# Layer 0 of a streaming encoder step: copying a chunk's first output part behind its first product, and reading sample states when their pair's values are made

## The chip, the cores and the metric

The kernel runs on one core of one Trainium2 chip. The metric is the time of one launch in microseconds (us) of device time, as the median of several runs. Engines are named as in the profile: PE is the matrix engine (PEld its weight loads), DVE the vector engine, ACT the scalar engine, POOL GpSimd, and SP the engine whose queue issues the DMAs.

## The reference, cut to what matters

Two layers are computed for 512 prompt tokens and 32 sample tokens. Layer 0 mixes tokens with RWKV-7: each of 24 heads keeps a 64 x 64 state that is updated token by token.

```
def step(S, inp):
    r_t, k_t, v_t, w_t, kk_t, a_t = inp
    sa = jnp.einsum('bhvk,bhk->bhv', S, -kk_t)
    S = (S * w_t[:, :, None, :] + sa[..., None] * (kk_t * a_t)[:, :, None, :]
         + v_t[..., None] * k_t[:, :, None, :])
    return S, jnp.einsum('bhvk,bhk->bhv', S, r_t)
xs = tuple(jnp.swapaxes(t, 0, 1) for t in (r, k, v, decay, kk, a))
S_T, y = lax.scan(step, S0.astype(f32), xs)
```

The prompt starts from a zero state, the sample from `state_rwkv`, one 64 x 64 matrix for each head. Both final states are outputs. Layer 1 is differential attention. Each layer has an input projection, a memory cross-attention, a gate and an output projection; these projections are most of the arithmetic.

## The kernel before, in words

**Tiling.** All tokens stand side by side as 544 columns (512 + 32). A projection block is 128 output columns: its weights are loaded (tiles `raw`), split into a high part by ACT (`whi`) and a low part by DVE (`wlo`), and multiplied in three products for each of 8 slices of the model dimension, over two halves of 272 columns (PSUM tile `ps_g`).

**The recurrence.** The 24 heads are 12 pairs; a pair fills the 128 partitions. The scan over tokens is replaced by chunks of 64 tokens: 8 prompt chunks in a row for a pair, and one sample chunk (number 8) with its own state. `rw_prep` makes the operands of a pair, `rw_values` the part of the chunks' values that needs no state (`avz`), `rw_chain` and `rw_sample` run the chunks through `chunk`, `rw_outputs` adds the rest of the outputs, `rw_finish` normalizes.

**A chunk**, with its PSUM tile `ps_c` (one bank, four parts), goes in three steps that follow each other through the engines; the names are those of the profile:

1. The first product `ps_c<-SB,zr` (PE) multiplies the state (`SB`, for the sample `ssi`) by the chunk's operands. One half of its rows is added by DVE to `avz` (`avz<-ps_c,avz`). The other half is the chunk's first output part.
2. The second product `ps_c<-avz,at` (PE) follows. ACT copies its result out in two copies (`sv<-ps_c`, for the sample `svs<-ps_c`), then copies the first output part of step 1 into the output tile (`yt<-ps_c`), then scales the old state (`sd<-SB,dl`).
3. The third product `ps_c<-sv,bt` (PE) and DVE's `SB<-ps_c,dl,sd` make the new state.

**Order.** Steps are Python generators. A hand-written table (`PLAN`, 23 rows of two halves) says in which place of a pair's chain the other steps of this and of neighbouring pairs are issued; between them the projection stream (`stream`) is filled in, a few matmuls at a time, so that PE has work while DVE and ACT finish a step. Each engine executes its instructions in the order in which the code issues them. In the plan, `rw_values` of pair p+1 is begun in row 22 of pair p and ended in row 1 of pair p+1; `rw_sample` is begun in row 5.

**The sample state.** The first thing that `rw_sample` does is to issue the two DMAs that read a pair's two matrices into the tile `SS`; right behind, in the same place of the plan, PE transposes `SS` (`ps_si<-ident,SS`), and DVE copies the result to `ssi`. After the sample chunk `SS` receives the new state, PE transposes it (`ps_so<-ident,SS`), and it is written out.

Of the kernel before, what the change touches and what calls it, by code (L numbers as in the profile page):

```python
# [108 lines left out]
class Trunk:  # L109
# [810 lines left out]
    H = [slice(0, 64), slice(64, P)]  # L920
# [8 lines left out]

    def rw_values(self, st):  # L930

        avz, H = self.avz, self.H
        for sets in (((0, 8),), ((1, 3, 5, 7), (2, 4, 6))):
            yield
            ps = [self.psm.tile([P, 4, P], F32, tag="m", name=f"ps_v{cs[0]}") for cs in sets]
            for j in range(len(sets[0])):
                for h in range(2):
                    for q, cs in zip(ps, sets):
                        if j < len(cs):
                            _, zs, ro, A, cv, _ = self.place(st, cs[j])  # L940
                            self.te.matmul(q[zs, j, H[h]], A[0][ro, h, :], cv[ro, H[h]], start=True, stop=True)
            for q, cs in zip(ps, sets):
                e, zs = self.place(st, cs[0])[:2]
                i = slice(0, 5, 4) if cs[0] == 0 else slice(cs[0] // 2, 4)
                self.ae.copy(avz[zs, e, i, :], q[zs, : len(cs)])
# [8 lines left out]
    def chunk(self, st, c, S, Snew):  # L954

        nc, H, yt = self.nc, self.H, st["yt"]
        e, zs, ro, A, cv, cb = self.place(st, c)
        i = c // 2
        yield
        ps = self.psc.tile([P, 4, P], F32, tag="c", name="ps_c")  # L960
        rhs = self.avz[:, e, i, :]
        sd = None
        if c:
            self.te.matmul(ps[:, 0, :], st["zr"][:, c * P : c * P + P], S[:], start=True, stop=True)
            self.ve.tensor_tensor(rhs[zs], ps[zs, 0, :], rhs[zs], ALU.add)
            yield

        self.te.matmul(ps[:, 1, :], A[0].rearrange("p h t -> p (h t)"), rhs, start=True, stop=True)
        for h in range(2):
            self.ae.copy(cv[zs, H[h]], ps[H[h], 1, H[h]])  # L970
        if c:
            self.ae.copy(yt[ro, i, :], ps[ro, 0, :])
            sd = self.rb2.tile([P, P], F32, tag="sd", name="sd", bufs=RB)
            self.ae.activation(sd[:], S[:], AF.Copy, scale=st["dl"][:, c : c + 1])
        yield
        self.te.matmul(ps[:, 2, :], cb, cv, start=True, stop=True)
        for hc in H:
            d = st["dl"][hc, c : c + 1]
            if c == 0:
                self.ve.tensor_scalar(Snew[hc, hc], ps[hc, 2, hc], d, None, ALU.mult)  # L980
            else:
                self.ve.scalar_tensor_tensor(Snew[hc, hc], ps[hc, 2, hc], d, sd[hc, hc], ALU.mult, ALU.add)
# [11 lines left out]
    def rw_sample(self, st):  # L994

        nc, p, pr = self.nc, self.rb2, st["pr"]
        sl = self.SS[0]
        for h in range(2):
            self.se.dma_start(sl[64 * h : 64 * h + 64, 64 * h : 64 * h + 64], self.a["state_rwkv"][0, 0, 2 * pr + h])
        yield  # L1000
        ps = self.psm.tile([P, 4, P], F32, tag="m", name="ps_si")
        self.te.transpose(ps[:, 0, :], sl[:], self.ident[:])
        S = p.tile([P, P], F32, tag="ssi", name="ssi", bufs=1)
        self.ve.tensor_copy(S[:], ps[:, 0, :])
        yield from self.chunk(st, 8, S, sl)
        yield
        self.state_out(sl, self.o[8][0, 0, 2 * pr : 2 * pr + 2])
# [1241 lines left out]
```

## Time and profile before

| | |
|---|---|
| median of 3 runs | 1373.17 us (1372.61 to 1374.08) |
| the profiled execution | 1373.67 us |
| its span in the trace | 1371.9 us, so 1.8 us lie around it |
| PE busy | 1343.1 us |
| PEld busy | 1289.0 us |
| DVE busy | 932.7 us |
| ACT busy | 827.6 us |
| POOL busy | 379.0 us |

The profile is of one execution. Layer 0's chunks lie between 133 and 660 us of the span. Row times in a timeline are the start from the span's beginning in us and then the duration in us; in brackets stands the idle time of that engine ahead of the instruction and what ended it.

### The profile page before, as it was taken

The page shows a single profiled execution, that of the slowest core. Times are in us where ns is not written, and L with a number is a line of the kernel's source. Part 1 is how long each engine was busy: PE and PEld are TensorE (multiplying, and loading weights), DVE is VectorE, ACT ScalarE, POOL GpSimd, SP SyncE. Part 2 cuts the span into 40 slices and gives each one's busy share as a digit, 9 for nine tenths or more (in the row PEclk, how much of TensorE's full clock was granted, in tenths as well). Part 3 has the DMA queues.
Part 4 walks back from the last instruction along what each step waited for, and adds up shares of the span by engine and source line. Part 5 has one row for each costly group of instructions (what it writes and reads, how often), then busy time and mean ns, then how long its engine had stood idle before and what let it go on. Part 6 is the DMA issues. An engine that isn't in the chain of part 4 may idle for free.

```text
span 1371.9 us, 31923 instructions
## 1 busy us (share of the span) xinstructions
PE 1343.1 (98%) x11893; PEld 1289.0 (94%) x11893; DVE 932.7 (68%) x2345; ACT 827.6 (60%) x2304; POOL 379.0 (28%) x841
## 2 busy tenths in 40 slices
PE   8999999999999999999999999999999999999997
PEld 6988899999999998988999999999999999999997
DVE  5776788888888888667734666775567747667443
ACT  5766777877778777656433466654566536665222
POOL 2128667766686666600000120000000001002000
PEclk9999999999999999999999999999999999999999
DMA  6452322333323332432644463333333323332321
GB/s 221 145 142 70 77 68 60 94 86 74 88 68 84 92 83 65 138 91 74 199 140 122 145 194 93 97 102 86 101 94 94 89 82 93 98 97 78 93 79 72
DMA packets 264036, 139.45 MB, mean 102 GB/s; under 512 B 57721, under 2 KB 252802, under 8 KB 263882
## 3 DMA queue, kind: packets, MB, share of 16 engines
q1 hardware_dynamic: 263818, 137.41, 35.7%
q8 instruction: 94, 1.54, 0.5%
q14 instruction: 60, 0.49, 0.1%
q10 hardware_dynamic: 64, 0.02, 0.0%
HBM read 111.12 MB, written 22.91 MB: 98 GB/s over the span
## 4 chain that ended last, share of the span: by engine, by line
PE 87%; DVE 5%; ACT 3%; POOL 2%; issue 1%; DMA 1%; SPq 1%; DVEq 0%; ACTq 0%; POOLq 0%
PE ps_g L106 60%; PE ps_c L106 5%; PE ps_s L106 2%; PE ps_o L106 2%; PE ps_at L106 2%; PE ps_v L106 2%; PE ps_mo L106 1%; PE ps_mm L106 1%; PE ps_w L106 1%; PE ps_aT L106 1%; POOL tm L868 1%; POOL u L870 1%; PE ps_yc L106 1%; PE ps_mt L106 1%; PE ps_wa L106 1%
## 5 line engine op out<-in xcount | busy, mean ns | idle before, releaser
L106 PE MATMUL ps_g<-hh,whi 128*128 128x272 f32 x1808 | 539.6, 299 | 1.0 <-DVE ats L106 0.7
L106 PE MATMUL ps_g<-hh,wlo 128*128 128x272 f32 x1808 | 534.7, 296 | 1.6 <-DVE wlo L106 1.5
L106 PE MATMUL ps_g<-hl,whi 128*128 128x272 f32 x1808 | 532.5, 295 | 0.6 <-DVE hl L106 0.3
L106 PEld LDWEIGHTS ps_g<-hh,whi 128*128 128x128 f32 x1808 | 341.1, 189 | 5.1 <-DVE ats L106 0.9
L106 PEld LDWEIGHTS ps_g<-hh,wlo 128*128 128x128 f32 x1808 | 340.6, 189 | 4.7 <-DVE wlo L106 2.5
L106 PEld LDWEIGHTS ps_g<-hl,whi 128*128 128x128 f32 x1808 | 341.1, 189 | 2.8 <-DVE hl L106 1.3
L106 DVE TENSOR_TENSOR wlo<-raw,whi 128x512 fp32r<-128x512 f32 x314 | 220.0, 711 | 122.3 <-ACT whi L106 118.9
L106 ACT CAST whi<-raw 128x512 fp32r<-128x512 f32 x314 | 188.9, 619 | 108.5 <-PE ps_g L106 61.4
L868 POOL TENSOR_TENSOR tm<-u,m 102x84 f32<-102x84 f32 (+23 forms) x341 | 145.6, 427 | 117.1 <-DMA m<-sc 67.1
L870 POOL TENSOR_TENSOR u<-u,tm 102x84 f32<-102x84 f32 (+23 forms) x341 | 150.4, 441 | 26.6
L106 PE MATMUL ps_g<-hi,whi 128*128 128x272 f32 x512 | 148.9, 291 | 0.0
L106 PE MATMUL ps_g<-hi,wlo 128*128 128x272 f32 x512 | 147.5, 288 | 0.5 <-DVE wlo L106 0.5
L106 PE MATMUL ps_g<-lo,whi 128*128 128x272 f32 x512 | 147.4, 288 | 0.0
L1339 POOL TENSOR_TENSOR lo<-og,hi 128x544 fp32r<-128x544 f32 x8 | 13.2, 1651 | 359.6 <-ACT hi L106 359.1
L106 PEld LDWEIGHTS ps_g<-hi,wlo 128*128 128x128 f32 x512 | 96.4, 188 | 0.8 <-DVE wlo L106 0.7
L106 PEld LDWEIGHTS ps_g<-hi,whi 128*128 128x128 f32 x512 | 96.4, 188 | 0.0
L106 PEld LDWEIGHTS ps_g<-lo,whi 128*128 128x128 f32 x512 | 96.4, 188 | 0.0
L106 ACT ACTIVATE pt<-ps_s,snm 128x128 f32<-128x128 f32 (+3 forms) x96 | 50.9, 531 | 41.8 <-DVE snm L106 41.6
L1766 POOL TENSOR_TENSOR hl<-hn,hh 128x544 fp32r<-128x544 f32 x8 | 12.5, 1566 | 211.2 <-ACT hh L106 211.2
L106 DVE SCALAR_TENSOR_TENSOR SB<-ps_c,dl,sd 64x64 f32<-64x64 f32 x168 | 47.4, 282 | 26.4 <-PE ps_c L106 21.1
L106 ACT COPY sv<-ps_c 64x64 f32<-64x64 f32 x192 | 39.5, 206 | 32.8 <-PE ps_c L106 30.9
L106 ACT ACTIVATE sg<-ps_g 128x272 f32<-128x272 f32 x64 | 25.2, 394 | 41.1 <-PE ps_g L106 38.3
(402 smaller groups left out, 2576.9 us busy)
## 6 DMA issues: line engine op xcount, KB each, us to landing
raw<-in_rw_in_dram SPq DMA_DIRECT2D x114, 256.0 KB
raw<-in_df_in_dram SPq DMA_DIRECT2D x112, 256.0 KB
raw<-in_w_out_dram SPq DMA_DIRECT2D x64, 256.0 KB
oscr<-sg SPq DMA_DIRECT2D x16, 272.0 KB
lo<-oscr SPq DMA_DIRECT2D x16, 272.0 KB
m<-sc SPq DMA_DIRECT2D x33, 128.0 KB
raw<-in_w_mem_v_dram SPq DMA_DIRECT2D x16, 256.0 KB
kh<-kh SPq DMA_DIRECT2D x24, 136.0 KB
```

The lines of the kernel that those rows point to most:

```text
L106: return lambda *a, **k: self.trunk.tie(self, issue(*a, **k))
L868: nc.gpsimd.tensor_tensor(tm[:, :n, :wd], u3[:, :n, kx : kx + 1].to_broadcast(sh), m3[:, kx : kx + 1, kx + 1 :].to_broadcast(sh), ALU.mult)
L870: nc.gpsimd.tensor_tensor(u3[:, :n, kx + 1 :], u3[:, :n, kx + 1 :], tm[:, :n, :wd], ALU.add)
L1339: (self.nc.gpsimd if g % 2 and self.o1 else self.ve).tensor_tensor(lo[:], t, hi[:].bitcast(F32), ALU.subtract)
L1766: nc.gpsimd.tensor_tensor(self.hl[:, k, :], h[:], self.hh[:, k, :].bitcast(F32), ALU.subtract)
```

## The change

The change has two parts, and only moves instructions.

- The copy `yt<-ps_c` of the first output part is issued right behind DVE's `avz<-ps_c,avz` (step 1 of the chunk), ahead of the second product, where it stood behind the two `sv<-ps_c` copies. This concerns 96 copies: chunks 1 to 7 and the sample chunk of 12 pairs.
- The two DMAs of `SS` are issued at the beginning of `rw_values` of their pair, where they stood at the beginning of `rw_sample`.

```
     def rw_values(self, st):
 
-        avz, H = self.avz, self.H
+        avz, H, pr = self.avz, self.H, st["pr"]
+        for h in range(2):
+            self.se.dma_start(self.SS[0][H[h], H[h]], self.a["state_rwkv"][0, 0, 2 * pr + h])
         for sets in (((0, 8),), ((1, 3, 5, 7), (2, 4, 6))):
             yield
...
             self.te.matmul(ps[:, 0, :], st["zr"][:, c * P : c * P + P], S[:], start=True, stop=True)
             self.ve.tensor_tensor(rhs[zs], ps[zs, 0, :], rhs[zs], ALU.add)
+            self.ae.copy(yt[ro, i, :], ps[ro, 0, :])
             yield
 
         self.te.matmul(ps[:, 1, :], A[0].rearrange("p h t -> p (h t)"), rhs, start=True, stop=True)
         for h in range(2):
             self.ae.copy(cv[zs, H[h]], ps[H[h], 1, H[h]])
         if c:
-            self.ae.copy(yt[ro, i, :], ps[ro, 0, :])
             sd = self.rb2.tile([P, P], F32, tag="sd", name="sd", bufs=RB)
...
         sl = self.SS[0]
-        for h in range(2):
-            self.se.dma_start(sl[64 * h : 64 * h + 64, 64 * h : 64 * h + 64], self.a["state_rwkv"][0, 0, 2 * pr + h])
         yield
```

On PE the sequence of matmuls stays; what the second product waits for is another engine. In pair 0, second chunk, the list of PE's instructions with what each waits for changes so (`ps_b` and `ps_g` are other work; a wait is named by the engine, or the DMA queue, whose semaphore it reads):

```order
 L106 MATMUL ps_b<-r_1904,hs_508 128x32
 L106 MATMUL ps_g<-hh,whi 128x272
-L106 MATMUL ps_c<-avz,at_89 128x128 [waits DMAHW2_49,DVE_49]
+L106 MATMUL ps_c<-avz,at_89 128x128 [waits DMAHW2_49,Activation_49]
 L106 MATMUL ps_g<-hl,whi 128x272
 L106 MATMUL ps_g<-hh,wlo 128x272
```

The second product waited for DVE's addition; now it waits for an instruction of ACT.

On ACT the copies move past 2 to 8 other instructions each. In pair 10 the last two chunks of the chain stood so (`t1b`, `at`, `mq`, `mp`, `mpT`, `hi`, `whi` are copies and activations of other steps):

```order
L106 CAST whi<-raw 128x512 [waits DMAHW4_49]
L106 COPY t1b<-ps_w_9771 32x256 [waits PE_49]
L106 COPY t1b<-ps_w_9771 32x256
L106 ACTIVATE mq<-ps_g 128x272 [waits PE_49]
L106 COPY sv<-ps_c 64x64 [waits PE_49]
L106 COPY sv<-ps_c 64x64
L106 COPY yt_1689<-ps_c 64x128
L106 ACTIVATE sd<-SB_538,dl 128x128 [waits Activation_49]
L106 COPY mpT<-ps_mt_9816 128x2x256 [waits PE_49]
L106 CAST hi_9332<-lo_9333 128x544 [waits DMAHW5_49]
L106 ACTIVATE mp,mrs<-ps_mm,mnm 128x256 [waits DVE_49,Activation_49]
L106 COPY mpT<-ps_mt_9870 128x2x256 [waits PE_49]
```

and now stand so:

```order
L106 CAST whi<-raw 128x512 [waits DMAHW4_49]
L106 COPY yt_1689<-ps_c 64x128 [waits DVE_49]
L106 COPY t1b<-ps_w_9772 32x256 [waits PE_49]
L106 COPY t1b<-ps_w_9772 32x256
L106 ACTIVATE mq<-ps_g 128x272 [waits PE_49]
L106 COPY sv<-ps_c 64x64 [waits PE_49]
L106 COPY sv<-ps_c 64x64
L106 ACTIVATE sd<-SB_538,dl 128x128 [waits Activation_49]
L106 COPY mpT<-ps_mt_9816 128x2x256 [waits PE_49]
L106 CAST hi_9334<-lo_9335 128x544 [waits DMAHW7_49]
L106 ACTIVATE mp,mrs<-ps_mm,mnm 128x256 [waits DVE_49,Activation_49]
L106 COPY yt_1689<-ps_c 64x128 [waits DVE_49]
```

The first copy has passed `t1b` and `mq`; the second, that of the next chunk, stands right behind `mp` and ahead of the second `mpT`. Each waits for DVE by itself, where it had no wait of its own behind `sv`.

On SP, where pair 10's state is read, the DMAs stood so (`cmt`, `mhk`, `mhv`, `cmv` are loads of the memory attention, `lo` of the output projection):

```order
L106 DMA oscr_476<-sg_83 128x544
L106 DMA cmt<-in_cache_mem_k_dram 128x2x128
L106 DMA mhk<-mkv_176 128x256
L106 DMA mhv<-mkv_779 128x256
L106 DMA cmv<-in_cache_mem_v_dram 128x2x128
L106 DMA raw<-in_rw_in_dram 128x4x128 x2
L106 DMA lo_9333<-oscr_475 128x544
L106 DMA lo_9382<-oscr_475 128x544
L106 DMA SS<-in_state_rwkv_dram 64x64 x2
```

and now stand so:

```order
L106 DMA oscr_476<-sg_83 128x544
L106 DMA SS<-in_state_rwkv_dram 64x64 x2
L106 DMA cmt<-in_cache_mem_k_dram 128x2x128
L106 DMA mhk<-mkv_176 128x256
L106 DMA mhv<-mkv_779 128x256
L106 DMA cmv<-in_cache_mem_v_dram 128x2x128
L106 DMA raw<-in_rw_in_dram 128x4x128 x2
L106 DMA lo_9335<-oscr_475 128x544
L106 DMA lo_9384<-oscr_475 128x544
```

The read of `SS` has moved ahead of eight other transfers. In pairs 1 to 9 it has moved ahead of one pair of `raw` loads, in pair 5 also of the four loads of `lam`, in pair 11 ahead of one pair of `raw` loads and one write of `oscr`; in pair 0 the queue is the same.

More of the change, by code (lines that the diff above doesn't have):

```diff
@@ L930, in rw_values @@
     def rw_values(self, st):
-        avz, H = self.avz, self.H
+        avz, H, pr = self.avz, self.H, st["pr"]
+        for h in range(2):
+            self.se.dma_start(self.SS[0][H[h], H[h]], self.a["state_rwkv"][0, 0, 2 * pr + h])
         for sets in (((0, 8),), ((1, 3, 5, 7), (2, 4, 6))):
@@ L965, in chunk @@
             self.ve.tensor_tensor(rhs[zs], ps[zs, 0, :], rhs[zs], ALU.add)
+            self.ae.copy(yt[ro, i, :], ps[ro, 0, :])
             yield
@@ L971, in chunk @@
         if c:
-            self.ae.copy(yt[ro, i, :], ps[ro, 0, :])
             sd = self.rb2.tile([P, P], F32, tag="sd", name="sd", bufs=RB)
@@ L997, in rw_sample @@
         sl = self.SS[0]
-        for h in range(2):
-            self.se.dma_start(sl[64 * h : 64 * h + 64, 64 * h : 64 * h + 64], self.a["state_rwkv"][0, 0, 2 * pr + h])
         yield
```

## Prediction

> **What bounds the kernel now.** I read the page first: how busy each engine is, and the chain that ended last.
>
> ```profile
> span 1371.9 us, 31923 instructions
> PE 1343.1 (98%) x11893; PEld 1289.0 (94%) x11893; DVE 932.7 (68%) x2345; ACT 827.6 (60%) x2304; POOL 379.0 (28%) x841
> PE 87%; DVE 5%; ACT 3%; POOL 2%; issue 1%; DMA 1%; SPq 1%; DVEq 0%; ACTq 0%; POOLq 0%
> ```
>
> PE is busy for 1343.1 of 1371.9 us, and 87% of the last chain is PE. The change takes no instruction away, so it can only win or lose PE's idle time, 28.8 us in all. What of it hangs on the moved instructions, the view of waits tells (us in total, times, longest), for PE and for its weight loads (PEld), which are what a wait really holds.
>
> ```profile
> PE ps_c L106 <- ACT yt L106: 2.3, 6, 0.6
> PE ps_c L106 <- DVE avz L106: 0.6, 2, 0.4
> PE ps_si L106 <- DMA SS<-in_state_rwkv_dram: 0.6, 1, 0.6
> PEld ps_c L106 <- ACT yt L106: 3.9, 7, 0.8
> ```
>
> So a chunk's third product now waits for the copy `yt` in 7 of 96 chunks, 3.9 us in the loads, and the transposition of a sample state waits once for its DMA. That is everything that the change can take away. The durations of the instructions concerned, from the groups:
>
> ```profile
> L106 ACT COPY yt<-ps_c 64x128 f32<-64x128 f32 x96 | 24.9, 260 | 1.3
> L106 DVE TENSOR_TENSOR avz<-ps_c,avz 64x128 f32<-64x128 f32 x96 | 27.5, 287 | 12.2 <-PE ps_c L106 10.8
> ```
>
> **The copy, where it gains.** I went through the timelines of DVE, ACT and PEld around the chunks. Here is pair 11's first chunk with a first product, the longest of the seven waits.
>
> ```profile
> 617.60 0.28 DVE L106 TENSOR_TENSOR avz<-ps_c,avz 64x128 f32<-64x128 f32 x1 [1.18 <-PE ps_c L106]
> 619.19 0.47 ACT L106 ACTIVATE mp<-ps_mm,mnm 128x256 f32<-128x256 f32 x1 [2.00 <-DVE mnm L106]
> 620.90 0.42 ACT L106 COPY sv<-ps_c 64x64 f32<-64x64 f32 x2
> 621.33 0.26 ACT L106 COPY yt<-ps_c 64x128 f32<-64x128 f32 x1
> 621.64 0.30 PEld L106 LDWEIGHTS ps_c<-sv,bt 128*128 128x128 f32 x2 [0.77 <-ACT yt L106]
> ```
>
> The load starts 0.05 us after the copy's end (621.59): that is the price of a hand-over. In the new order the copy stands ahead of `mp`, in ACT's idle 2.00 us, and the third product waits only for `sv`, which ends at 621.32: it starts at 621.37, 0.27 earlier; the rest of the 0.77 stays, now behind `sv`. Three more of the seven (loads at 553.41, 577.30 and 640.91) have an ACT gap to take the copy too: 4 x 0.27 = 1.1 us won. In the other three ACT has no gap between the new place and `sv`; there the copy only changes places with `sv` in a full queue, `sv` ends when the copy ended, and nothing is won.
>
> **The copy, where it costs.** The order shows two new waits: the copy waits for DVE's addition, and the second product waits for the copy. Until now that product could start one hand-over after the addition; now 0.05 + 0.26 + 0.05 = 0.36 us after it, and later still if ACT is busy. Most chunks have the room: 0.1 to 1.8 us in pairs 1 to 8. Where they have not:
>
> ```profile
> 600.42 0.19 PEld L106 LDWEIGHTS ps_g<-hl,whi 128*128 128x128 f32 x1
> 600.55 0.31 PEld L106 LDWEIGHTS ps_c<-avz,at 128*128 128x128 f32 x2
> 632.94 0.19 PEld L106 LDWEIGHTS ps_c<-sv,bt 128*128 128x128 f32 x1 [0.58 <-ACT yt L106]
> 600.22 0.62 ACT L106 CAST whi<-raw 128x512 fp32r<-128x512 f32 x1
> 600.86 0.74 ACT L106 COPY t1b<-ps_w 32x256 f32<-32x256 f32 x2
> ```
>
> PE comes to the second product at 600.55 with no gap (its loads follow each other every 0.12 to 0.13). The copy will stand between `whi` and `t1b`, so it runs from 600.86 to 601.12, and the product starts at 601.17: 0.6 us lost. The same happens at 630.60, but there the third product waits 0.58 us anyway, and takes it up.
>
> The second kind of cost is ACT itself: it now stands still until DVE has added, and what is queued behind it is late.
>
> ```profile
> 137.54 0.28 DVE L106 TENSOR_TENSOR avz<-ps_c,avz 64x128 f32<-64x128 f32 x1
> 137.88 0.30 PEld L106 LDWEIGHTS ps_c<-avz,at 128*128 128x128 f32 x2 [0.44 <-DVE avz L106]
> 137.15 0.39 ACT L106 COPY raw<-ps_g 128x272 f32<-128x272 f32 x1
> 138.40 0.42 ACT L106 COPY sv<-ps_c 64x64 f32<-64x64 f32 x2 [0.23 <-PE ps_c L106]
> 139.20 0.32 PEld L106 LDWEIGHTS ps_c<-sv,bt 128*128 128x128 f32 x2
> ```
>
> The addition ends at 137.82; the second product moves from 137.88 to 138.18. ACT, which would begin `raw` at 137.15, waits until 137.87, copies, and begins `raw` at 138.15, 1.0 late; 0.23 of that is taken up by its idle time ahead of `sv`, so `sv` ends at 139.6 instead of 138.82, and the third product starts at 139.65: 0.45 lost.
>
> ```profile
> 157.85 0.28 DVE L106 TENSOR_TENSOR avz<-ps_c,avz 64x128 f32<-64x128 f32 x1 [0.28 <-PE ps_c L106]
> 157.75 0.73 ACT L106 ACTIVATE bv<-bv,PA 128x544 f32<-128x544 f32 x1
> 160.20 0.30 PEld L106 LDWEIGHTS ps_c<-sv,bt 128*128 128x128 f32 x2 [0.24 <-ACT yt L106]
> ```
>
> Here, the first of the seven waits, ACT runs without a gap from `bv` to `yt`. `bv` would start at 158.46 instead of 157.75, all behind it is 0.7 late, and the third product, which now is spared 0.28, is still 0.4 late. The same at 546.9: 0.5.
>
> ```profile
> 606.57 0.58 ACT L106 COPY mpT<-ps_mt 128x512 f32<-128x512 f32 x1 [0.75 <-PE ps_mt L106]
> 607.18 0.28 DVE L106 TENSOR_TENSOR avz<-ps_c,avz 64x128 f32<-64x128 f32 x1
> 607.33 0.74 ACT L106 COPY at<-ps_w 32x256 f32<-32x256 f32 x2 [0.18 <-PE ps_w L106]
> 608.52 0.30 PEld L106 LDWEIGHTS ps_v<-sv,at 64*64 64x64 f32 x4
> 528.55 0.30 PEld L106 LDWEIGHTS ps_c<-sv,bt 128*128 128x128 f32 x2 [0.74 <-ACT yt L106]
> ```
>
> DVE comes late to this addition. `mpT` goes from 606.57 to 607.79, `at` ends at 609.1 instead of 608.07, and `ps_v`, which reads `at`, starts at 609.15: 0.6 lost. By the same working 0.4 at 625.3, 0.2 at 542.6, 0.2 at 645 and 650 together, and nothing at 526.4 (0.3, taken up by a third product that waits 0.74). Sum of these places: 0.6 + 0.45 + 0.4 + 0.5 + 0.6 + 0.4 + 0.2 + 0.2 = 3.4 us.
>
> The middle pairs repeat each other, so a small loss there counts several times. The tightest place, in pair 4:
>
> ```profile
> 341.77 0.27 DVE L106 TENSOR_TENSOR avz<-ps_c,avz 64x128 f32<-64x128 f32 x1
> 341.61 0.49 ACT L106 ACTIVATE ta<-ps_wa,dv 128x272 f32<-128x272 f32 x1 [0.63 <-PE ps_wa L106]
> 342.62 0.74 ACT L106 COPY at<-ps_w 32x256 f32<-32x256 f32 x2 [0.52 <-PE ps_w L106]
> 342.50 0.30 PEld L106 LDWEIGHTS ps_c<-avz,at 128*128 128x128 f32 x2
> 343.55 0.30 PEld L106 LDWEIGHTS ps_v<-sv,at 64*64 64x64 f32 x4
> ```
>
> The copy runs from 342.09 to 342.35, so the second product at 342.50 keeps its time. `ta` moves from 341.61 to 342.37, `at` from 342.62 to 342.87, 0.25 late; PE uses `at` 0.19 after its end (343.55 against 343.36), of which 0.05 is the hand-over. That leaves 0 to 0.1 lost in each of seven pairs; I take half, 0.35.
>
> The Trainium skill, page "PSUM — Partial Sum Buffer", section "PSUM bank collisions raise a hardware error", wants semaphores by bank and quadrant of 32 partitions: two engines may use one bank at once in different quadrants. The copy and DVE's addition read different halves of the partitions, so by that rule the copy need not wait for the addition, and all that I price as ACT standing still would go; the sum would be about 1.5 us lower. The order shows the wait, so it is paid here. The second product writes all partitions of the same bank, and its wait for the copy agrees with the rule.
>
> **The sample state.** The two DMAs are SP's; what matters is where PE waited:
>
> ```profile
> 562.43 0.37 SPq L106 DMA_DIRECT2D cmt<-in_cache_mem_k_dram  x1
> 567.35 1.12 SPq L106 DMA_DIRECT2D SS<-in_state_rwkv_dram  x2
> 572.05 0.14 PEld L106 LDWEIGHTS ps_si<-ident,SS 128*128 128x128 f32 x1 [0.73 <-PE ps_c L106]
> ```
>
> In pair 10 the read is issued at 567.35 behind eight transfers, and PE waits for it at 572.05. In the new order it is issued at 562.43, 4.9 us sooner: the 0.6 us are won. In the other pairs PE never waited for it. The price is that what it passed goes 1.12 us later; as the weights are loaded two blocks ahead and no wait of PE for a `raw` is in the view above, I put it at nothing; were that cover gone, it would be up to 1.1 us at one of ten places. The tile is free in time, as the old state leaves it in the row of the plan before. The Trainium skill, page "SBUF — State Buffer", section "The DMA setup-cost knee", gives a transfer a fixed cost of about 2 us; by it the state would have been there at 570.5, before PE came, and the gain would be nothing. The row decides: 3.6 us passed from the end of the issue to the load.
>
> **Sum.** 3.4 + 0.35 - 1.1 - 0.6 = +2.05 us. Half the losses lie close together at the end of layer 0, and a PE that is already late finds ACT's copy done more often; I take 0.5 off: +1.5. Behind 660 us the change touches nothing, so it is handed on as it is. The profiled execution took 1373.67 us (1.8 around its span), so 1375.2; the median of the runs is 0.5 below that execution: 1374.7.
>
> **Bounds.** Best: no second product loses anything and all seven third products are spared the copy, 7 x 0.27 + 0.6 = 2.5 us won, 1370.7. Worst: no gain, all losses, 0.1 in all seven pairs, and the passed loads: 3.4 + 0.7 + 1.1 = 5.2, 1378.4.
>
> **Rivals.** First, slower by over 0.2%: ACT's standing still paces the middle pairs. In nine pairs about four of eight copies find ACT ready 0.3 to 0.75 us before DVE has added, and ACT hands on the delay. If each costs PE 0.1 us, 36 x 0.1 = 3.6 comes on top: 1378.3. For it speaks that the plan is tight in the rows of pair 4; against it, that third products there come 0.5 to 1.5 us after `yt`. It decides from 0.04 us for each copy. Second, the costs are taken up by waits that PE has anyway, and only the gains stay: 1373.2 - 1.7 = 1371.5. For it speak the places 526.4 and 630.6; against it, the six where PE had no gap. Third, faster by over 0.2%: `sv` itself would have to come earlier, so that the 3.9 us of the loads go altogether, with the 0.6: 1368.7. Nothing in the queues moves `sv` forward. Fourth, the copy does not wait where the order says; then it is the best bound, 1370.7.
>
> **Chances.** About 0.2% (2.7 us) is what a measurement here can tell from no change. My forecast, between no change and 0.2% slower: 0.58; second rival and the like, up to 0.2% faster: 0.15; first rival, slower: 0.20; third and fourth: 0.07, mostly within reach of 0.2%. So faster 0.06, same 0.74, slower 0.20. The range, 1371.3 to 1377.6, takes in the second rival and half of the first, and leaves 0.07 + 0.10 = 0.17 outside.
>
> **What would show it.** In the new profile the waits of `ps_c` for `yt` should fall to a part of 3.9 us but not go, now at the second product, and `ps_c` should wait for `sv`; ACT's `yt` should have idle time of 10 us or more ahead of it with `avz` as what ended it, where it now has 1.3; `ps_si` should wait for no DMA. `ps_v` should begin about 0.1 later against `at`'s old place in pairs 1 to 7. I am wrong if the middle pairs, 44 us each, change by over 0.2 us, or if `raw` or `wlo` appears among PE's new waits.

## The result, and the profile after

| | before | changed |
|---|---|---|
| median of 19 runs | 1373.09 us (1370.93 to 1375.84) | 1374.89 us (1374.33 to 1376.31) |
| the profiled execution | 1373.67 us | 1374.87 us |
| its span | 1371.9 us | 1373.2 us |

The ratio is 1.0014, with a 95% interval of 1.0008 to 1.0020: the change costs 1.1 to 2.7 us. The prediction was 1374.7, 1.5 above before.

The page of the changed kernel: span, busy times and chain.

```profile
span 1373.2 us, 31921 instructions
PE 1345.1 (98%) x11893; PEld 1290.1 (94%) x11893; DVE 931.4 (68%) x2345; ACT 831.9 (61%) x2304; POOL 382.5 (28%) x841
PE 88%; DVE 5%; ACT 3%; DMA 2%; issue 1%; POOL 1%; SPq 1%; DVEq 0%; POOLq 0%; ACTq 0%
```

Nothing in these lines shows what happened. The waits do (us in total, times, longest):

```profile
PEld ps_c L106 <- ACT yt L106: 3.6, 6, 0.9
PEld ps_c L106 <- ACT sv L106: 2.1, 7, 0.5
PEld ps_bt L106 <- ACT svs L106: 0.9, 2, 0.5
ACT yt L106 <- DVE avz L106: 65.5, 63, 2.7
```

PE's wait for `yt` is almost as long as before (3.6 against 3.9 us), but it stands at other instructions: six second products. The old one, at the third products, has shrunk to 2.1 us and now hangs on `sv`. `ps_bt` waits for `svs`, which it did not. ACT stands still ahead of 63 of the 96 copies until DVE has added, 65.5 us in all; only a small part of that reaches PE. `ps_si` waits for no DMA any more.

**Where the time went.** PE's loads come in the same order in both kernels. So each load's start in the new trace less its start in the old one (the *drift*) tells where time is lost or won. I count from the first chunk's third product in pair 0, ahead of every moved copy, to the last third product in pair 11. First the two rows of before, then those of after.

```profile
134.65 0.31 PEld L106 LDWEIGHTS ps_c<-sv,bt 128*128 128x128 f32 x2
658.30 0.30 PEld L106 LDWEIGHTS ps_c<-sv,bt 128*128 128x128 f32 x2
...
134.87 0.32 PEld L106 LDWEIGHTS ps_c<-sv,bt 128*128 128x128 f32 x2
659.68 0.30 PEld L106 LDWEIGHTS ps_c<-sv,bt 128*128 128x128 f32 x2
```

The drift goes from +0.22 to +1.38: the change costs 1.16 us in this pair of executions, and behind 660 us it stays between +1.2 and +1.4. The 0.22 stand ahead of every moved copy, and so are not the copies'. Between the rows lie 523.65 us before and 524.81 after; this length is used for all kernels below, as it leaves out the start and layer 1.

### The profile page after: what moved, and what is told of

Read it like the earlier page. It is cut to its first block, busy times and chain, and to the rows that moved or that the text cites. A ratio compares the mean times of both kernels' runs of the same rounds, so it can differ in the third digit from the quotient of the medians.

```text
span 1373.2 us, 31921 instructions
## 1 busy us (share of the span) xinstructions
PE 1345.1 (98%) x11893; PEld 1290.1 (94%) x11893; DVE 931.4 (68%) x2345; ACT 831.9 (61%) x2304; POOL 382.5 (28%) x841
## 4 chain that ended last, share of the span: by engine, by line
PE 88%; DVE 5%; ACT 3%; DMA 2%; issue 1%; POOL 1%; SPq 1%; DVEq 0%; POOLq 0%; ACTq 0%
PE ps_g L106 61%; PE ps_c L106 6%; PE ps_s L106 2%; PE ps_o L106 2%; PE ps_at L106 2%; PE ps_v L106 2%; PE ps_mo L106 1%; PE ps_mm L106 1%; PE ps_w L106 1%; DVE wlo L106 1%; PE ps_aT L106 1%; PE ps_yc L106 1%; PE ps_wa L106 1%; PE ps_kv L106 1%; PE ps_q L106 1%
## 5 line engine op out<-in xcount | busy, mean ns | idle before, releaser
L106 ACT COPY yt<-ps_c 64x128 f32<-64x128 f32 x96 | 24.9, 259 | 67.0 <-DVE avz L106 65.5
```

The source lines that it names most:

```text
L106: return lambda *a, **k: self.trunk.tie(self, issue(*a, **k))
```

## The experiments

The length is counted as above, against 523.65 us. "Step" is the change of the drift at one place. Ratios are to the kernel before in the same session, with their 95% intervals; its medians there were 1373.09 us (changed), 1373.37 (e1 to e4), 1373.50 (e5 to e8) and 1373.47 (e9 to e11). e4, e6 and e9 ran 4 times, e8 5 times, the other experiments 11 times. e3 to e11 all have the early reads of SS.

| kernel | median, us | ratio | length |
|---|---|---|---|
| changed | 1374.89 | 1.0014 (1.0008 to 1.0020) | +1.16 |
| e1: SS part alone | 1372.90 | 0.9999 (0.9990 to 1.0007) | -0.87 |
| e2: copy part alone | 1375.07 | 1.0014 (1.0006 to 1.0023) | +1.61 |
| e3: copies of pairs 0, 9 to 11 | 1374.82 | 1.0011 (1.0002 to 1.0020) | +0.81 |
| e10: copies of pairs 1 to 8 | 1372.98 | 0.9996 (0.9987 to 1.0005) | -0.46 |
| e5: four gaining copies | 1372.24 | 0.9995 (0.9986 to 1.0004) | -1.19 |
| e6: copy ahead of the addition | 1388.18 | 1.0108 (1.0094 to 1.0122) | +13.21 |
| e9: copy one row later | 1428.30 | 1.0400 (1.0384 to 1.0416) | +53.51 |
| e4: five copies held back | 1387.06 | 1.0100 (1.0084 to 1.0115) | +12.79 |
| e8: four copies held back | 1378.69 | 1.0042 (1.0029 to 1.0055) | +4.61 |
| e7: six copies moved | 1372.89 | 1.0000 (0.9991 to 1.0009) | -0.72 |
| e11: three copies moved | 1372.07 | 0.9989 (0.9981 to 0.9998) | -1.61 |

### The two parts apart (e1, e2)

e1 takes the diff of the copy back, e2 that of the DMAs.

```
e1:  self.te.matmul(ps[:, 1, :], ...)  ... sv copies
     if c:
+        self.ae.copy(yt[ro, i, :], ps[ro, 0, :])      # as before
e2:  def rw_values(self, st):
-        for h in range(2):
-            self.se.dma_start(self.SS[0][H[h], H[h]], ...)   # again in rw_sample
```

> The change's second part alone: the two reads of SS are issued at the beginning of rw_values, the copies yt stay behind the two sv copies. Theory: the wait of pair 10's transposition for SS goes, and nothing else moves: 0.6 to 0.8 us faster than before (about 1372.4), ps_si waits for no DMA, and the ps_c loads still wait 3.9 us for yt. Rival A (what the reads have passed comes late): a wait of PE for whi or wlo of up to 1.1 us comes in its place, and the time is before's or above. Rival B (the wait was hidden by another one): within 0.2 us of before.

> The change's first part alone: the copy yt is issued right behind DVE's addition, the reads of SS stay at the beginning of rw_sample. Theory: the costs of the copy stand alone, 1.8 to 2.2 us slower than before (about 1375.1), with the 0.6 us wait of ps_si for the DMA as in before, and the waits of the ps_c loads for yt now at the second product. Rival (the loss in the changed kernel comes from the reads of SS and what they passed): not slower than before.

Both as the theory had it in the traces; the median of e1 alone does not tell it from before. The rows of the transposition in pair 10, in the changed kernel and then in e2:

```profile
573.09 0.14 PEld L106 LDWEIGHTS ps_si<-ident,SS 128*128 128x128 f32 x1
...
572.74 0.14 PEld L106 LDWEIGHTS ps_si<-ident,SS 128*128 128x128 f32 x1 [0.19 <-PE ps_c L106]
```

Before, this load had 0.73 us of idle time ahead of it; in e1 and in the changed kernel that is gone, with a step of -0.81. In e2 the read is issued where it was, but only 0.19 is left of the wait, with a step of -0.54: PE, late from the copies, arrives 0.54 later against the read than before, and the wait takes that up. So the early read saves 0.8 us where PE is in time, and 0.3 beside the copies: the two parts overlap.

### Where the copies cost (e3, e10)

```
-            self.ae.copy(yt[ro, i, :], ps[ro, 0, :])
+            if not 1 <= st["pr"] <= 8:      # e3; e10: if 1 <= st["pr"] <= 8
+                self.ae.copy(yt[ro, i, :], ps[ro, 0, :])
             yield
...
+            if 1 <= st["pr"] <= 8:          # the others where they were
+                self.ae.copy(yt[ro, i, :], ps[ro, 0, :])
```

> Both parts, but the copy is issued early only in pairs 0, 9, 10 and 11; in pairs 1 to 8 it stays behind the sv copies. Theory: the loss lies in the four pairs where PE comes to a second product without a gap or ACT has work queued behind the copy; the time is that of the changed kernel within 0.2 us (about 1374.8), and the middle pairs, 88 us for two, keep their length within 0.1 us. Rival (ACT's standing still costs a little in each of the 64 middle copies): 1 us or more faster than the changed kernel.

> The reads of SS as in the change; the copy yt is issued early only in pairs 1 to 8, and behind the sv copies in pairs 0, 9, 10 and 11. Theory: the middle pairs have room for it, 0 to 0.3 us in all, so the time is that of the SS part alone, about 1373.0, and PE's loads drift by no more than 0.3 us between pair 1 and pair 8. Rival (0.1 us for each copy that finds ACT waiting, the prediction's first rival): 3 us slower than the SS part alone.

Most of the loss is in the 32 copies of pairs 0, 9, 10 and 11: against e1, the length grows by 1.7 us in e3 and by 0.4 in e10, and by 2.0 with all copies. The first rival, 3.6 us from the middle pairs, is out: the median of e10 is that of the SS part alone (1372.98 and 1372.90). Across pairs 1 to 8 the drift grows by 0.27 (changed), 0.21 (e2) and 0.29 us (e10) with early copies there, and by 0.08 (e1), -0.35 (e3), -0.14 (e5) and 0.06 (e11) without. That is some 0.3 us, hardly more than executions differ by: e3 moves none of these copies, and yet its -0.35 lies beyond the 0.1 that I had expected.

### The gains alone (e5)

```
+EARLYC = ((9, 6), (10, 2), (11, 1), (11, 4))     # (pair, chunk)
-            self.ae.copy(yt[ro, i, :], ps[ro, 0, :])
+            if (st["pr"], c) in EARLYC:
+                self.ae.copy(yt[ro, i, :], ps[ro, 0, :])
```

> The reads of SS as in the change; the copy yt is issued early only in the four chunks that the prediction priced as gains (pair 9 chunk 6, pair 10 chunk 2, pair 11 chunks 1 and 4), and behind the sv copies in the other 92. Theory: these four third products each come 0.27 us earlier, but at pair 9 chunk 6 and pair 11 chunk 4 the next wait (the state addition, ps_mm for mq) takes it back, so 0.5 us are won beside the 0.5 of the SS part alone: about 1372.3, 1 us below before, and 2.5 below the changed kernel. Rival (the early copy costs at those places too): like the SS part alone, or slower.

The steps at the four third products are -0.26, -0.23, -0.28 and -0.27 us, as expected, and two are given back: +0.38 at the next state product in pair 9, +0.26 at `ps_mm` in pair 11. The same places in the changed kernel, and behind the dots the two loads that took the gain, as they were before:

```profile
554.97 0.30 PEld L106 LDWEIGHTS ps_c<-sv,bt 128*128 128x128 f32 x2 [0.21 <-ACT sv L106]
555.41 0.81 DVE L106 TENSOR_TENSOR wlo<-raw,whi 128x512 fp32r<-128x512 f32 x1
556.24 0.58 DVE L106 SCALAR_TENSOR_TENSOR SB<-ps_c,dl,sd 64x64 f32<-64x64 f32 x2
556.87 0.30 PEld L106 LDWEIGHTS ps_c<-SB,zr 128*128 128x128 f32 x2 [0.44 <-DVE SB L106]
...
641.87 0.30 PEld L106 LDWEIGHTS ps_c<-sv,bt 128*128 128x128 f32 x2 [0.28 <-ACT sv L106]
642.72 0.73 PEld L106 LDWEIGHTS ps_mm<-mhk,mq 128*128 128x128 f32 x4 [0.55 <-ACT mq L106]
...
555.03 0.30 PEld L106 LDWEIGHTS ps_c<-SB,zr 128*128 128x128 f32 x2 [0.16 <-DVE SB L106]
641.49 0.73 PEld L106 LDWEIGHTS ps_mm<-mhk,mq 128*128 128x128 f32 x4 [0.29 <-ACT mq L106]
```

At 556.87 the wait for `SB` is 0.44, where it was 0.16 (0.28 longer in the changed kernel): `SB` stands behind `wlo` in DVE's queue and starts when `wlo` is done (556.22), so the earlier third product does not bring it forward. At 642.72 the wait for `mq` is 0.55, where it was 0.29. At both places the gain ends at the next wait for an engine that the change did not make earlier.

### Who goes first, and where in ACT's queue (e6, e9)

```
e6:
+            self.ae.copy(yt[ro, i, :], ps[ro, 0, :])
             self.ve.tensor_tensor(rhs[zs], ps[zs, 0, :], rhs[zs], ALU.add)
-            self.ae.copy(yt[ro, i, :], ps[ro, 0, :])
             yield
e9:
-            self.ae.copy(yt[ro, i, :], ps[ro, 0, :])
             yield
+        if c:
+            self.ae.copy(yt[ro, i, :], ps[ro, 0, :])
         self.te.matmul(ps[:, 1, :], ...)
```

> As the changed kernel, but the copy yt is issued ahead of DVE's addition, not behind it. The two read the same bank, and the program makes the second wait for the first in either order: here DVE waits for ACT. Theory (the cost of the change is the two in a row, not who goes first): ACT no longer stands still for DVE, but the addition, and with it the second product, comes 0.3 us later wherever ACT is free, and more where ACT is busy (at the second product that the prediction saw move from 600.55 to 601.17, to 601.45); DVE stands still, and wlo with it. 1.5 to 4 us slower than before, about 1375.7. Rival (ACT's standing still was the cost): 1 us or more below the changed kernel.

> As the changed kernel, but the copy yt is issued one row of the plan later, right ahead of the second product: on ACT it now stands behind the 1 to 9 instructions of that row, directly ahead of the sv copies, and the second product still waits for it. It parts the two costs. Theory (both count, and the second product's wait is the larger one): ACT no longer stands still for DVE, so pair 0 and pair 9 lose nothing at chunk 5 (ps_bt does not wait for svs), but the second product waits for all that ACT has in front of the copy; in the middle pairs, whose room is 0.1 to 1.8 us, that costs 0.3 to 0.8 us a pair: 3 to 8 us slower than before, about 1378. Rival (ACT's standing still is the whole cost): 1 us or more below the changed kernel, about 1373.5.

The direction is the theory's in both, the size is not: 14.7 us instead of 1.5 to 4, and 55 instead of 3 to 8. The waits of e6, then of e9:

```profile
DVE avz L106 <- ACT yt L106: 47.5, 67, 2.5
PEld ps_c L106 <- DVE avz L106: 6.6, 14, 1.1
PE ps_at L106 <- DVE bk L106: 7.1, 10, 0.8
...
PEld ps_c L106 <- ACT yt L106: 61.5, 64, 2.2
```

In e6 DVE stands still 67 times. Besides the second products (6.6 us) that makes `bk` late, and PE's matmul `ps_at` waits for it once in each of pairs 0 to 9: 7.1 us in 10, where before it was 0.5 us in 1. I had looked at the chunk's own products alone. In e9 the second product waits 64 times, almost 1 us each: ACT's instructions of the same row of the plan stand ahead of the copy, and ACT works them off at about the time when PE arrives. `ps_bt` has no step any more in pairs 0 and 9, as expected. One of the 64 places, ACT and then PE:

```profile
377.81 0.75 ACT L106 ACTIVATE rkv<-raw,dv 128x544 f32<-128x544 f32 x1
378.59 0.19 ACT L106 COPY raw<-PC 128x1 f32<-128x1 f32 x1
378.69 0.25 ACT L106 COPY yt<-ps_c 64x128 f32<-64x128 f32 x1
378.99 0.30 PEld L106 LDWEIGHTS ps_c<-avz,at 128*128 128x128 f32 x2 [0.90 <-ACT yt L106]
```

The load comes 0.05 behind the copy's end, and 0.90 us after PE was ready. So ACT's standing still in the changed kernel is the cheaper of the two ways: the copy waits for DVE 65.5 us in all (65.9 in e2), but 1.6 us reach the end (e2).

### Held copies (e4, e8, e7, e11)

The third way is to hold the copy until the next chunk's second product, so that neither product of its own chunk waits for it.

```
+LATE = (1, 3, 4, 5, 6)                  # e8: (3, 4, 5, 6)
+        if c < 8 and self.held:
+            self.held.pop()()            # the last chunk's copy
         self.te.matmul(ps[:, 1, :], ...)
...
+            first = lambda: self.ae.copy(yt[ro, i, :], ps[ro, 0, :])
+            if c in LATE: self.held.append(first)
+            else: first()
e7:  early (10, 2), (11, 1); held (0, 5), (9, 6), (11, 3), (11, 4)
e11: early (10, 2), (11, 1); held (0, 5)      # (pair, chunk)
```

> The reads of SS as in the change; the copy yt of chunks 1, 3, 4, 5 and 6 is not issued early but held back, and issued in the next chunk right ahead of its second product (the tile has two buffers); chunks 2, 7 and the sample keep the old place behind sv. Theory: neither the second nor the third product of those chunks waits for a copy, so the third product waits for sv alone; where the long waits were, 0.27 us each go, a part of which is given back at the state addition and at ps_mm: 0.5 to 1.5 us faster than the SS part alone, about 1371.5. Rival A (the held copy stands in ACT's way at its new place and delays the next chunk's sv): like the SS part alone or slower. Rival B (sv comes when it comes, and the wait for it stays): no more than 0.2 us from the SS part alone.

> As the kernel with the held copies that was 13.7 us slower, but chunk 1's copy is not held: only those of chunks 3, 4, 5 and 6 are. Theory (chunk 1's held copy keeps one of the two buffers of ps_c, which the sample chunk's first product needs next; its lateness of 0.84 us comes back as 0.63 us at chunk 4, which needs the sample's buffer): both losses go, and the time is 1371.5 to 1372.5. Rival (the 0.63 us at chunk 4 come from chunk 3's held copy): some 0.6 us in each of ten pairs stay, about 1379.

> The reads of SS as in the change; the copy yt is moved in six chunks alone: early in pair 10 chunk 2 and pair 11 chunk 1, held until the next chunk's second product in pair 0 chunk 5, pair 9 chunk 6 and pair 11 chunks 3 and 4. Theory: none of the six third products waits for the copy any more, and sd, which follows sv at once, comes earlier too: 0.27 us each, so 1.6 us less what other waits take back (0.6), beside the 0.5 of the SS part: about 1371.9. Rival: within 0.3 us of the SS part alone (1372.9), since other waits take it all back.

> The reads of SS as in the change; the copy yt is moved in three chunks alone, where no other wait took the gain back: early in pair 10 chunk 2 and pair 11 chunk 1, held until the next chunk's second product in pair 0 chunk 5. Theory: 0.8 us at the state's transposition, 0.22 + 0.28 + 0.25 us at the three third products, no loss: 1.4 us below before by the loads' drift, about 1372.0. Rival (the held copy keeps a buffer that chunk 6 of pair 0 needs): like the SS part alone or slower.

e4 lost 13.7 us. The theory had a gain; rival A allowed a loss, but from the copy standing in ACT's way, and none had asked until when a held copy keeps its buffer. The rows name the place: the sample's first product waits for the held copy of chunk 1 (ACT's copy, then PE's load, in pair 4).

```profile
318.58 0.26 ACT L107 COPY yt<-ps_c 64x128 f32<-64x128 f32 x1
318.89 0.30 PEld L107 LDWEIGHTS ps_c<-ssi,zr 128*128 128x128 f32 x2 [0.77 <-ACT yt L107]
```

That is a step of 0.84 us in most pairs, and e8, with chunk 1's copy back in its place, does not have it. But the second loss, 0.63 us at chunk 4, stays in e8, which took 1378.69 us and not 1372.5 or less: the rival was right on it. Before (first two rows) and e8:

```profile
323.59 0.60 DVE L106 SCALAR_TENSOR_TENSOR SS<-ps_c,dl,sd 64x64 f32<-64x64 f32 x2
323.67 0.30 PEld L106 LDWEIGHTS ps_c<-SB,zr 128*128 128x128 f32 x2 [0.27 <-PE ps_g L106]
...
325.45 0.60 DVE L107 SCALAR_TENSOR_TENSOR SS<-ps_c,dl,sd 64x64 f32<-64x64 f32 x2
326.20 0.46 PE L107 MATMUL ps_c<-SB,zr 128*128 128x128 f32 x2 [0.71 <-DVE SS L107]
```

Before, chunk 4's product starts while DVE still reads the sample's bank (323.59 to 324.19): it has taken the other buffer, chunk 3's. In e8 chunk 3's buffer is held by its copy, so chunk 4 gets the sample's, and waits until `SS` is done (326.05). In turn, chunk 4 would have had the sample's buffer before as well; so the rows read as if a buffer is taken when it comes free, and a late reader changes which one the next chunk gets. The rows carry no buffer numbers, so this is inferred.

e7 holds chunk 3 in pair 11 and loses 0.62 at the next chunk's first product; its gain at pair 9 goes back as in e5. Its median, 1372.89, is the rival's and not the 1371.9 of the theory. e11 keeps only the places where no other wait took the gain: steps of -0.81 at the state, -0.27 at pair 0 chunk 5, -0.18 and -0.27 at the two early copies. It is below before in its whole interval, by 0.02% to 0.19%, and some 3 us below the changed kernel (ratios 0.9989 and 1.0014).

## Why the prediction was right, point by point

The total was right (+1.5 predicted, +1.16 in the length, +1.8 in the medians). The terms, with the steps of the changed kernel's drift:

| place (time before) | priced | step | what happened |
|---|---|---|---|
| 137.88, 139.20 | +0.45 | +0.45 - 0.37 | as priced; what goes at 145.12, where `ps_at` waits for `bk`, differs by execution (below) |
| 157 to 160 | +0.4 | +0.43 | as priced, but held by `ps_bt`, one load earlier |
| pairs 1 to 8 | +0.35 | +0.27 | near in size, the priced place not (below) |
| 526.40 | 0 | +0.31 - 0.30 | taken up, as priced |
| 542.63 | +0.2 | +0.2 | as priced |
| 546.9 | +0.5 | +0.6 | nearly as priced, most of it at `ps_bt` (547.66) |
| 553.41 | -0.27 | 0 | won, then lost to `SB` |
| 572.05 | -0.6 | -0.81 | won; 0.54 of it also without the early read |
| 577.30, 621.64 | -0.54 | -0.51 | as priced |
| 600.55 | +0.6 | +0.48 - 0.48 | taken up at 602.76 and by `ps_y` |
| 607 | +0.6 | +0.30 | half (below) |
| 625.32 | +0.4 | +0.30 | nearly as priced |
| 630.60, 632.94 | 0 | +0.60 - 0.59 | taken up, as priced |
| 640.91 | -0.27 | 0 | won, then lost to `mq` |
| 645, 650 | +0.2 | +0.31 | nearly as priced |
| overlap | -0.5 | in the rows above | |

The mechanism stands: the losses and gains came where the copy was put on a wait or taken off one. That the total fits so well is in part luck. Priced losses of 0.9 us did not reach the end (600.55 and half of 607), two gains of 0.27 did not stay, and the 0.5 taken off for overlap made up the difference. The reason given for it, that a late PE finds ACT's copy done more often, no run isolates.

The step at 145.12 differs from execution to execution. Up to and with it, the drift grows by 0.12 (changed), 0.43 (e2) and 0.30 (e3) where pair 0's copies are early, and moves by -0.31 (e1), -0.11 (e10), +0.02 (e5), -0.22 (e8), -0.15 (e7) and -0.15 (e11) where the copies up to there stand as before. Between the two means lies 0.43 us, so about the priced 0.45 is lost there, and the +1.16 may be some 0.3 too low.

Pair 0's first place, and from 158.53 its second, in the changed kernel:

```profile
138.07 0.26 ACT L106 COPY yt<-ps_c 64x128 f32<-64x128 f32 x1 [0.71 <-DVE avz L106]
138.36 0.39 ACT L106 COPY raw<-ps_g 128x272 f32<-128x272 f32 x1
138.38 0.30 PEld L106 LDWEIGHTS ps_c<-avz,at 128*128 128x128 f32 x2 [0.73 <-ACT yt L106]
139.87 0.30 PEld L106 LDWEIGHTS ps_c<-sv,bt 128*128 128x128 f32 x2
...
158.53 0.26 ACT L106 COPY yt<-ps_c 64x128 f32<-64x128 f32 x1 [0.35 <-DVE avz L106]
158.81 0.75 ACT L106 ACTIVATE bv<-bv,PA 128x544 f32<-128x544 f32 x1
159.85 0.26 ACT L106 COPY svs<-ps_bts 32x128 f32<-32x128 f32 x1
160.16 0.42 PEld L106 LDWEIGHTS ps_bt<-ident,bk 128*128 128x128 f32 x4 [0.53 <-ACT svs L106]
```

Copy, then `raw`, then everything behind it late; the second product 0.05 behind the copy. Behind the copy at 158.53 `bv` is late, `svs` with it, and `ps_bt` waits.

**The term at 600.55 was mis-sized.** The second product came 0.48 later, but the loss was gone 4 us on:

```profile
601.61 0.26 ACT L106 COPY yt<-ps_c 64x128 f32<-64x128 f32 x1
601.92 0.30 PEld L106 LDWEIGHTS ps_c<-avz,at 128*128 128x128 f32 x2 [0.43 <-ACT yt L106]
605.09 0.53 PEld L106 LDWEIGHTS ps_y<-ident,yt 128*128 128x128 f32 x5
...
604.20 0.53 PEld L106 LDWEIGHTS ps_y<-ident,yt 128*128 128x128 f32 x5 [0.37 <-issue]
604.24 0.74 PE L106 MATMUL ps_y<-ident,yt 128*128 128x128 f32 x5 [0.18 <-DVE yt L106]
```

Before (last two rows), `ps_y` had idle time ahead of it until DVE's `yt`; now it has almost none. The third product at 602.76 took 0.16 and `ps_y` 0.32. I had looked for such a wait at 630.60 and not here.

**The term at 607 was mis-sized by a reading.** I let `at` end at 608.07, the end of a row that is marked x2, and `ps_v` begin behind that. The rows after:

```profile
608.69 0.30 PEld L106 LDWEIGHTS ps_c<-avz,at 128*128 128x128 f32 x2 [0.41 <-ACT yt L106]
609.27 0.74 ACT L106 COPY at<-ps_w 32x256 f32<-32x256 f32 x2
609.70 0.30 PEld L106 LDWEIGHTS ps_v<-sv,at 64*64 64x64 f32 x4
```

`ps_v` begins at 609.70, while the second of the two copies still runs (to 610.01): it needs the first alone. It comes 1.01 us after the second product, as before (608.52 less 607.51). The 0.30 are the second product's own. The same mistake stands in the middle pairs. The place in pair 4, in the changed kernel:

```profile
343.87 0.74 ACT L106 COPY at<-ps_w 32x256 f32<-32x256 f32 x2
344.54 0.30 PEld L106 LDWEIGHTS ps_v<-sv,at 64*64 64x64 f32 x4
```

`ps_v` comes 0.99 later than before at a drift of 1.0, so it lost nothing, though `at` begins 1.25 later; the 0.27 came in small steps elsewhere, within what executions differ by.

**The signs in the profile.** `yt` waits for `avz` (65.5 us, where I had said 10 or more), `ps_c` waits for `sv`, the wait for `yt` did not go (it fell by 0.3 us only), the state waits for no DMA, no `raw` or `wlo` is among the new waits, and of the middle pairs only pair 1 changes by as much as 0.2 us (+0.21, the others by 0.11 at most). The guess for `ps_v` was wrong. Of the other rivals, the second has its mechanism in the places that are taken up, but not its time; the third and the fourth are out, as `sv` still makes PE wait 2.1 us and the copy waits for DVE 63 times.

**The rules of the pages.** The Trainium skill, page "PSUM — Partial Sum Buffer", section "PSUM bank collisions raise a hardware error", lets two engines share a bank in different quadrants. Here the program orders the two readers whichever is issued first (e6: DVE waits 47.5 us for ACT), so the row decided; whether the chip would allow them together no run here shows. The page "SBUF — State Buffer", section "The DMA setup-cost knee", would have given the early read no gain; PE's load of the state has a step of -0.81 us in e1, so the row of 3.6 us was the better guide. How much of the 3.6 us was the eight transfers ahead in the queue, no run here takes apart.

**What stays open.** The medians give +1.8 and the length +1.16; the interval (1.1 to 2.7) holds both. With the 0.3 us of 145.12 the two come closer, but the runs do not tell which is nearer.

## What to carry to other kernels

A copy that is taken off one wait is put on another: ask which instruction now waits for it, what stands behind it in its engine's queue, and until when it keeps its buffer; the same copy cost +1.2, +13 and +54 us in three places a few instructions apart. A gain or a loss of 0.3 us lives only until the next wait for another engine, so follow it there before adding it up. Moving three of 96 copies, those that earlier traces showed to gain and keep it, beside the early read, which is half of the gain, was worth more than moving all.

## What the runs showed that I had not expected

At most places the drift's steps repeat from kernel to kernel within a few hundredths: at 630.60 they are +0.60 (changed), +0.61 (e2) and +0.60 (e3), at 572.05 -0.81 in the changed kernel, e1, e3, e5, e10 and e11. 145.12 is the exception (-0.37 in the changed kernel, -0.05 in e2). One profiled execution of each kernel so resolves 0.3 us at most places, where the medians of 11 runs leave an interval some 0.0017 of the time wide, 2.3 us. The start of the kernel does not repeat so: at 60 us the drift was -0.97 in the changed kernel and +0.46 in e1, ahead of any edit, and at 134.65 it was +0.22 and -0.53.
